# Two attentions with all products over 128 rows and contiguous operands, and rows of maxima turned on DVE

## The chip, the core and the metric

The kernel runs on one core of a Trainium2 chip. The core has a matrix engine (TensorE; PE in the profile, PEld for its weight loads), a vector engine (DVE), a scalar engine (ACT), a third elementwise engine (POOL) and SP, which only issues DMAs here. Each works through its own instructions in order and waits for the others by semaphores. A matmul multiplies a stationary operand (its weights, loaded by an instruction of its own) by a moving one and writes to a PSUM bank of 128 x 512 float32. The metric is the time of one execution in microseconds on the device; lower is better.

## What is computed

Two layers of an encoder over 512 tokens of width 1024, all in float32. Each layer runs two attentions beside a pooling branch, gates and merges the three, and ends with a gated MLP of width 2816. What matters here are the attentions:

```python
def block_attention(q, k, v):
    ...
    scale = dk ** -0.5
    ...
    def one_block(qi):
        sc = jnp.einsum('bqgrd,bkgd->bgrqk', qi, k, preferred_element_type=jnp.float32) * scale
        p = jax.nn.softmax(sc, axis=-1).astype(v.dtype)
        return jnp.einsum('bgrqk,bkgv->bqgrv', p, v)
...
    # MLA: 8 heads of 64 + 32 features, keys' 32 rotary features shared by the heads
    q = jnp.concatenate([q[..., :MLA_NOPE], apply_rope(q[..., MLA_NOPE:], cos, sin)], axis=-1)
    k = jnp.concatenate([k[..., :MLA_NOPE], apply_rope(k[..., MLA_NOPE:], cos, sin)], axis=-1)
    o = block_attention(q, k, v)
    # GQA: 8 heads of 64 features over 2 heads of keys and values
    q = apply_rope(rms_norm(q, qn_g), cos, sin)
    k = apply_rope(rms_norm(k, kn_g), cos, sin)
    o = block_attention(q, k, v)
```

GQA stands for the grouped-query attention and MLA for the latent one. So there are 16 heads a layer, each with a softmax over 512 keys for 512 queries.

## The kernel before, in words

**Precision.** TensorE works on a rounded form of float32 (the type fp32r). So an operand is split into a high part, written by ACT, and a low part, the difference, by DVE or POOL; a full product is the sum of three matmuls. Splitting the weights (`wh`, `wl` out of `raw`, 512 columns a piece) is most of POOL's work.

**Order.** The program writes the order of every engine's instructions out by hand. While it is built it keeps a clock (`Clock`) with a guessed cost for every instruction; `chain` puts the steps of a piece of work one behind the other in that clock, and `need` lets it run on until a result is ready. The clock decides nothing on the chip: it fixes which instruction stands before which on an engine, and in places which engine takes a piece (`pick`, `copy`). A changed cost of one step can so move other instructions too. Semaphores guard every true dependence.

**Stages.** In each layer the projections come first, then the GQA attention, then the MLA attention, then the output projection and the MLP. Products that don't depend on the attention (gates, branch projections, MLA's own q, k, v) are fed in between the attention's products as a filler, from a list in which each step of each head has its position (`PLAN`; four units are one head). `s_max` of a head stands up to about two units before its `probs`.

**A head.** Features lie over the rows (partitions), tokens over the 512 columns.

- `t_q`, `t_k` make the high and low parts of queries and keys. For GQA, `qa` holds the high part of a query head in its 64 rows and the low part in the other 64, `ka` the keys' high part twice, `kb` the keys' low part in rows 0 to 63 and ones in row 64, `qb` the queries' high part in rows 0 to 63. For MLA all are 96 rows high; `ka` has ones in row 96.
- `s_max` multiplies, for each of four blocks of 128 queries, the queries (as weights, every fourth column of `qa`) by all keys into the one bank `S`, and `red` on DVE takes the negative maximum over the keys into a column of `nm` (128 x 4). When the fourth is there, `row` moves the 512 numbers into one row of 512: row 64 of `qb` (GQA) or row 96 of `qa` (MLA), by a DMA issued from ACT's queue. The row of ones in the keys then subtracts the maximum inside the product of the scores.
- `probs`, for each of four blocks of 128 keys, makes the scores in a bank `ST` or `mi`: two matmuls for GQA (over 128 and 65 rows), three for MLA (96, 96 and 97 rows). Then come the exponential (ACT), the split into `ph` and `pl`, and a small rest (`vt`).
- `av_hi`, `av_lo`, `av_rest` multiply by the values into a bank `AV`; `o_out` normalizes.

**Turns.** MLA's queries and keys are made with tokens over the rows and must be turned. `block_turn` turns blocks of 32x32 on DVE (`turn_blocks`), writes them to DRAM (`put`) and reads them back in order (`get`: three DMAs of 64 KB for 96 features), both issued by SP. `mla_turn` does so for one head's queries (`tq`) or keys (`tk`); SP's queue carries the weights (`raw`) as well. The first turns of MLA are issued when the GQA attention has been written out.

**Buffers.** Most intermediate tiles are slots of 128 x 512 out of a ring of 47 (`slot`); small ones have buffers of their own (`small`).

Of the kernel before, what the change touches and what calls it, by code (L numbers as in the profile page):

```python
# [14 lines left out]
ALU = mybir.AluOpType  # L15
# [29 lines left out]
PLAN = {"gqa": (-4.2, -1.0, -0.2, 0.0, 0.65, 2.411, 4.57, 32.003),  # L45
        "mla": (-6.2, -2.9, -1.0, 0.1, 0.64, 1.678, 1.82, 35.5)}

D_ROW, D_OUT, D_IN, D_LAT = 3.4, 3.2, 4.0, 6.0
REST = 0.4
W_BIAS = 2.54  # L50
C_BIAS = 0.2
# [200 lines left out]


@with_exitstack
def trunk(ctx: ExitStack, tc: tile.TileContext, x, w, prm, gb, cst, out):
    nc = tc.nc
    ctx.enter_context(tc.manual_schedule())
    ck = Clock()
# [24 lines left out]
    def small(name, shape, dt=F32, bufs=2):  # L283
        uid[0] += 1
        t = sm.tile(shape, dt, tag=name, name=f"{name}_{uid[0]}", bufs=bufs)
        return t
# [22 lines left out]
    def f(ap):  # L309
        return ap.bitcast(F32)  # L310
# [226 lines left out]
    def layer(l, sq, xsrc):  # L537
# [12 lines left out]
        gcol = small("gcol", [P, 1], bufs=1)  # L550

        def tables():
            V.tensor_tensor(gcol[0:96], pr[0:96, PRM_MQ:PRM_MQ + 1], pr[0:96, PRM_MQ + 1:PRM_MQ + 2], ALU.mult)
            V.tensor_scalar(gcol[0:64], gcol[0:64], 96.0 ** -0.5, None, ALU.mult)
            V.tensor_scalar(gt[:, 0:128], gt[:, 0:128], 64.0 ** -0.5, None, ALU.mult)
            V.tensor_scalar(gt[:, 256:384], gt[:, 256:384], 96.0 ** -0.5, None, ALU.mult)
            for tb, o in zip(tabs, (0, 128)):
                for i, c0 in ((0, C_CG), (1, C_SG)):
                    G.tensor_tensor(
                        tb[:, 256 * i:256 * i + 256].rearrange("p (b f) -> p b f", b=4),  # L560
                        C[:, c0:c0 + 256].rearrange("p (b f) -> p b f", b=4),
                        bc(gt[:, None, o + 64 * i:o + 64 * i + 64], [P, 4, 64]), ALU.mult)
# [173 lines left out]
        def set_ones():  # L736
            for vh, _ in VG:
                V.memset(f(vh[:, :, 64:65]), 1.0)
            for _, kb in KAB:
                V.memset(f(kb[64:65, :T]), 1.0)  # L740

        at(14.0, set_ones)
# [190 lines left out]
        vm0 = small("vm0", [P, 4, 8])  # L933
        ss = small("ssm", [P, 2, 2, 4, 4])
        krr = small("krr", [P, 4, 32], bufs=1)
        kj_ = small("kj", [P, 4, 32], bufs=1)
        kss = small("kss", [P, 4], bufs=1)

        def rotary():
# [153 lines left out]

        turned = {}

        def block_turn(what, h, srcs, n):


            tr, to = slot("tr"), slot("tf")
            turned[what, h] = to  # L1100
            d = dp.tile([P, P * n], F32, tag=f"d{what}{l}{h}", name=f"d{what}{l}{h}")
            o = tr[:, :P * n].rearrange("p (j b t) -> p b j t", j=n, b=4)

            def turn_blocks():
                for b0, nb, src in srcs:
                    V.transpose(o[:, b0:b0 + nb], src.rearrange("p b (j f) -> p b j f", f=32))

            def put():
                SY.dma_start(d, tr[:, :P * n])
                ck.fin = ck.now + D_OUT  # L1110

            def get():
                for j in range(n):
                    SY.dma_start(to[32 * j:32 * j + 32, :T].rearrange("f (i c) -> f i c", i=4),
                                 d.rearrange("(i f) (j c) -> j f i c", i=4, j=n)[j])
                ck.fin = ck.now + D_IN
                done(what, l, h)

            return turn_blocks, put, get

        def mla_turn(what, h):
            m = (MQ if what == "tq" else MK)[h // 4]
            chain(([("mq" if what == "tq" else "mk", l, h // 4)], lambda: None),
                  *block_turn(what, h, [(0, 4, m[:, :, h % 4, :])], 3), after=0.0)


        def attention(kind, fill, okey, odst):
            gqa = kind == "gqa"
            hs, ot = {}, []
            kd = P if gqa else 96  # L1130

            def key(*k):
                return (kind, l) + k
# [1 line left out]
            def t_q(h):  # L1135
                if gqa:
                    return t_pair(h) if h % 2 == 0 else None
                s = hs.setdefault(h, {})
                need(("tq", l, h))
                qf = turned.pop(("tq", h))  # L1140
                qa, qb = s["qa"], s["qb"] = slot("qa", F32R), slot("qb", F32R)

                def lo():
                    G.tensor_tensor(qb[0:96, :T], qf[0:96, :T], f(qa[0:96, :T]), ALU.subtract)
                    done(*key("q", h))

                chain(lambda: A.activation(qf[0:96, :T], qf[0:96, :T], AF.Copy, scale=gcol[0:96]),
                      lambda: A.activation(qa[0:96, :T], qf[0:96, :T], AF.Copy), lo, after=0.0)

            def t_pair(h):  # L1150

                if h:
                    need(("tp", l, h))
                    tp = turned.pop(("tp", h))[:, :T]
                else:
                    tp = ps("mi")
                    for b in range(4):
                        need(("gqn", l, b))
                        turn(tp[:, b * P:b * P + P], gqo[b][:, :P])
                need(("kab", l))  # L1160
                steps = []
                for i in range(2):
                    s = hs[h + i] = {}
                    s["ka"], s["kb"] = KAB[h // 4]
                    qa, qb = s["qa"], s["qb"] = slot("qa", F32R), slot("qb", F32R)
                    own, other = slice(64 * i, 64 * i + 64), slice(64 - 64 * i, P - 64 * i)

                    def hi(qa=qa, own=own):
                        A.activation(qa[own, :T], tp[own], AF.Copy)

                    def lo(i=i, qa=qa, qb=qb, own=own, other=other):
                        (G if h else V).tensor_tensor(qa[other, :T], tp[own], f(qa[own, :T]), ALU.subtract)
                        if i == 1 and h == 0:
                            free("mi")
                        A.activation(qb[0:64, :T], qa[own, :T], AF.Copy)
                        done(*key("q", h + i))

                    steps.append((hi, lo))
                chain(steps[0][0], steps[1][0], steps[0][1], steps[1][1])
# [11 lines left out]
            def t_k(h):  # L1191
                if gqa:
                    return
                s = hs.setdefault(h, {})
                need(("tk", l, h))
                kf = turned.pop(("tk", h))
                ka, kb = s["ka"], s["kb"] = slot("kh", F32R), slot("kl", F32R)

                def hi():
                    G.memset(f(ka[96:97, :T]), 1.0)  # L1200
                    A.activation(ka[0:96, :T], kf[0:96, :T], AF.Copy)
                    done(*key("kh", h))

                def lo():
                    G.tensor_tensor(kb[0:96, :T], kf[0:96, :T], f(ka[0:96, :T]), ALU.subtract)
                    done(*key("kl", h))

                chain(hi, lo, after=0.0)

            def s_max(h, b):  # L1210
                s = hs[h]
                need(key("q", h))
                if not gqa:
                    need(key("kh", h))
                if b == 0:
                    s["nm"] = small("nm", [P, 4], F32R)
                sc = ps("S")
                mm(sc, s["qa"][0:kd, b:T:4], s["ka"][0:kd, :T], True, True)

                def red():  # L1220
                    V.tensor_reduce(s["nm"][:, b:b + 1], sc, AX.X, ALU.max, negate=True)
                    free("S")

                def row():
                    nc.scalar.dma_start(f((s["qb"][64:65] if gqa else s["qa"][96:97])[:, :T]), f(s["nm"]))
                    ck.fin = ck.now + D_ROW
                    done(*key("m", h))

                chain(red, *[row] * (b == 3))

            def probs(h, k):
                s = hs[h]
# [5 lines left out]
                kb_ = slice(k * P, k * P + P)  # L1238
                if gqa:
                    mm(sc, s["ka"][:, kb_], s["qa"][:, :T], True, False)  # L1240
                    mm(sc, s["kb"][0:65, kb_], s["qb"][0:65, :T], False, True)
                else:
                    mm(sc, s["kb"][0:96, kb_], s["qa"][0:96, :T], True, False)
                    mm(sc, s["ka"][0:96, kb_], s["qb"][0:96, :T], False, False)
                    mm(sc, s["ka"][0:97, kb_], s["qa"][0:97, :T], False, True)
                ph, pl = slot("ph", F32R), slot("pl", F32R)
                s["p", k] = (ph, pl)

# [477 lines left out]
```

## Time and profile before

| | |
|---|---|
| runs | 1580.4, 1580.51, 1582.9 us; median 1580.51 |
| the profiled execution | 1580.47 us, of it 1578.5 from the first to the last instruction (its span) |
| GQA attention, first and second layer | 106 to 238 us, 889 to 1021 us |
| MLA attention | 238 to 350 us, 1021 to 1132 us |
| DMA | 164.43 MB, 104 GB/s on the mean |

In the rows of the profile a group reads: line, engine, operation, written tile <- read tiles (for a matmul the moving operand, then the weights' tile), shapes, count | busy us in all, mean ns of one | idle us of the engine just before, and what ended it. The line is often that of a helper that records all operations of a kind. A matmul's duration counts its way through the array; the next one starts before it ends, so that 512-wide matmuls follow each other at some 0.23 us. A row of a timeline has the start and the length in us, then the instruction, and in brackets the idle time before it and what ended it. Stretches are listed as start and end, length, busy time (and number of instructions) of PE, PEld, DVE, ACT and POOL, granted clock, share of the DMA engines, GB/s.

### The profile page before, as it was taken

The numbers are of one execution on the slowest core, as the hardware profiler recorded it, in microseconds if no ns is written. First come the engines' busy times: TensorE is split into PE (matmuls) and PEld (weight loads), VectorE is DVE, ScalarE is ACT, GpSimd is POOL, SyncE is SP. The second block draws the span as 40 slices with busy tenths as digits, with TensorE's granted clock in tenths as the row PEclk, the third lists the DMA queues.
The fourth block names the chain that finished last, engine by engine and source line by source line (L and its number), as shares of the span: only waits on it lengthen the run. The fifth ranks groups of instructions, "written<-read, shape, count | busy, mean of one in ns | idle before, by whom it ended". The sixth has DMA issues, their size and how long they took to land.

```text
span 1578.5 us, 20363 instructions
## 1 busy us (share of the span) xinstructions
PE 1566.6 (99%) x7098; PEld 1310.3 (83%) x7098; DVE 952.9 (60%) x1360; ACT 787.4 (50%) x1426; POOL 1021.1 (65%) x890
## 2 busy tenths in 40 slices
PE   9999999999999999999999999999999999999999
PEld 8888888888888888888898888888888888888888
DVE  6877967866267776721047788678652777777000
ACT  6367866663444444432244677576534444444221
POOL 3864986854667667654577649868547766676542
PEclk9999999999999999999999999999999999999999
DMA  5432234314333233333334322343242223223331
GB/s 200 124 107 81 78 93 134 117 54 140 107 94 100 94 98 96 102 108 124 106 100 129 106 74 78 102 139 104 68 152 94 90 96 102 94 96 105 120 113 48
DMA packets 85927, 164.43 MB, mean 104 GB/s; under 512 B 25025, under 2 KB 47041, under 8 KB 85825
## 3 DMA queue, kind: packets, MB, share of 16 engines
q1 hardware_dynamic: 80928, 162.93, 33.3%
q8 instruction: 56, 0.92, 0.2%
q10 hardware_dynamic: 4896, 0.21, 0.2%
q14 instruction: 47, 0.38, 0.1%
HBM read 149.41 MB, written 13.63 MB: 103 GB/s over the span
## 4 chain that ended last, share of the span: by engine, by line
PE 87%; DVE 4%; POOL 2%; ACT 2%; issue 2%; DMA 2%; SPq 1%; POOLq 0%; ACTq 0%
PE ps_acc L367 39%; PE ps_AV L367 21%; PE ps_ST L367 21%; PE ps_S L367 3%; PE ps_mi L367 3%; DVE XM L223 1%; POOL wl L223 1%; DVE mgl L223 1%; ACT mgh L216 1%; POOL win L223 1%; SPq L713 1%; DVE gt L227 0%; DMA tf<-dtq 0%; ACT wh L216 0%; DMA tf<-dl 0%
## 5 line engine op out<-in xcount | busy, mean ns | idle before, releaser
L223 POOL TENSOR_TENSOR wl<-raw,wh 128x512 fp32r<-128x512 f32 (+2 forms) x503 | 674.2, 1352 | 413.3 <-ACT wh L216 374.4
L216 ACT ACTIVATE wh<-raw 128x512 fp32r<-128x512 f32 (+1 forms) x521 | 308.5, 607 | 124.8 <-PE ps_ST L367 42.0
L227 DVE SCALAR_TENSOR_TENSOR a<-u,prm,a 128x511 f32<-128x511 f32 x176 | 242.5, 1379 | 89.2 <-ACT a L216 84.3
L367 PE MATMUL ps_acc<-HH,wh 128*128 128x512 f32 x592 | 231.9, 392 | 0.5 <-DVE gt L223 0.5
L367 PE MATMUL ps_acc<-HH,wl 128*128 128x512 f32 x592 | 231.3, 391 | 0.0
L367 PE MATMUL ps_acc<-HL,wh 128*128 128x512 f32 x592 | 231.3, 391 | 0.0
L367 PEld LDWEIGHTS ps_acc<-HH,wl 128*128 128x128 f32 x592 | 111.3, 188 | 23.6
L367 PEld LDWEIGHTS ps_acc<-HH,wh 128*128 128x128 f32 x592 | 111.6, 188 | 23.0 <-issue 0.9
L367 PEld LDWEIGHTS ps_acc<-HL,wh 128*128 128x128 f32 x592 | 111.4, 188 | 22.9
L367 PE MATMUL ps_AV<-HH,wh 128*128 128x512 f32 x288 | 112.4, 390 | 0.0
L367 PE MATMUL ps_AV<-HH,wl 128*128 128x512 f32 x288 | 112.2, 390 | 0.0
L367 PE MATMUL ps_AV<-HL,wh 128*128 128x512 f32 x288 | 112.2, 390 | 0.0
L223 POOL TENSOR_TENSOR al<-a,ah 128x512 fp32r<-128x512 f32 x44 | 57.9, 1316 | 83.5 <-ACT ah L216 78.8
L231 DVE TENSOR_REDUCE nm<-ps_S 128x1 fp32r<-128x512 f32 x128 | 87.7, 685 | 37.5 <-PE ps_S L367 35.6
L367 PE MATMUL ps_ST<-HH,wh 128*128 128x512 f32 x240 | 93.7, 390 | 0.0
L367 PE MATMUL ps_ST<-HL,wh 128*128 128x512 f32 x240 | 93.5, 390 | 0.0
L367 PE MATMUL ps_ST<-HH,wl 128*128 128x512 f32 x240 | 93.5, 389 | 0.0
L216 ACT ACTIVATE ah<-a 128x512 fp32r<-128x512 f32 x44 | 27.8, 632 | 127.8 <-DVE a L223 127.8
L216 ACT ACTIVATE a<-u,prm 128x512 f32<-128x512 f32 x88 | 71.0, 809 | 27.0 <-DVE u L223 26.5
L216 ACT ACTIVATE a<-a 128x512 f32<-128x512 f32 x44 | 27.8, 632 | 106.2 <-DVE a L227 106.2
L216 ACT ACTIVATE HH<-XM,prm 128x512 fp32r<-128x512 f32 x32 | 23.1, 722 | 104.4 <-DVE XM L223 53.9
L216 ACT ACTIVATE ps_ST<-ps_ST 128x512 f32<-128x512 f32 x86 | 49.9, 581 | 39.8 <-PE ps_ST L367 38.0
(376 smaller groups left out, 3734.1 us busy)
## 6 DMA issues: line engine op xcount, KB each, us to landing
raw<-w SPq DMA_DIRECT2D x228, 512.0 KB, 3.5
raw<-w SPq DMA_DIRECT2D x13, 384.0 KB, 3.1
XM<-x SPq DMA_DIRECT2D x16, 256.0 KB, 4.2
dtq<-tr SPq DMA_DIRECT2D x16, 192.0 KB, 3.9
dtk<-tr SPq DMA_DIRECT2D x16, 192.0 KB, 4.0
tf<-dtq SPq DMA_DIRECT2D x48, 64.0 KB, 2.1
tf<-dtk SPq DMA_DIRECT2D x48, 64.0 KB, 2.4
raw<-w SPq DMA_DIRECT2D x6, 448.0 KB, 3.4
```

The costliest lines, as they stand in the source:

```text
L216: return self.eng.activation(out, in_, func, **k)
L223: return self.eng.tensor_tensor(out, *a)
L227: return self.eng.scalar_tensor_tensor(out, *a)
L231: return self.eng.tensor_reduce(out, in_, *a, **k)
L367: PE.matmul(o, lhsT=lhsT, rhs=rhs, start=start, stop=stop)
L713: SY.dma_start(to[32 * c:32 * c + 32, :T].rearrange("f (g t) -> f g t", t=32), src[4 * j + c])
```

## The change

- Contiguous weights: block b of `s_max` takes the 128 neighbouring columns b*128 to b*128+127 of `qa` in place of every fourth one.
- Full rows: every product of the attentions runs over 128 rows. The rows that had not been there are filled: for MLA the turns read 32 more rows from a new input `pad` (zeros for queries; a row of ones and 31 of zeros for keys) by one more DMA each, and all passes over 96 rows become passes over 128, where `gcol`, the scale per row, is first set to 1; the memset of the row of ones in `ka` goes. For GQA, rows 64 to 127 of `kb` are zeroed once a layer ahead of the ones, and rows 64 to 127 of `qb` by a memset on POOL for each head.
- Row of maxima: `lie` turns `nm`, each number repeated 32 times, in blocks of 32x32 on DVE into `nmt` (128 x 128), so that every group of 32 rows holds 128 of the maxima on each row; then `row` copies the four groups to 32 rows of `qb` or `qa`, two on ACT and two on DVE. The DMA is gone; all 32 rows hold the maxima, and only one of them meets a key row that isn't zero.
- `kj`, a small tile, becomes a slot; the clock's constant for the DMA goes.

```diff
-D_ROW, D_OUT, D_IN, D_LAT = 3.4, 3.2, 4.0, 6.0
+D_OUT, D_IN, D_LAT = 3.2, 4.0, 6.0
...
+            V.memset(gcol, 1.0)
...
+                V.memset(f(kb[64:P, :T]), 0.0)
                 V.memset(f(kb[64:65, :T]), 1.0)
...
-        kj_ = small("kj", [P, 4, 32], bufs=1)
+        kj_ = slot("kj2")[:, :P].rearrange("p (b f) -> p b f", b=4)
...
-        def block_turn(what, h, srcs, n):
+        def block_turn(what, h, srcs, n, rest=None):
...
+                if rest is not None:
+                    SY.dma_start(to[32 * n:P, :T], rest)
                 ck.fin = ck.now + D_IN
...
-            m = (MQ if what == "tq" else MK)[h // 4]
+            m, rest = (MQ[h // 4], pad[0]) if what == "tq" else (MK[h // 4], pad[1])
...
-                    G.tensor_tensor(qb[0:96, :T], qf[0:96, :T], f(qa[0:96, :T]), ALU.subtract)
+                    G.tensor_tensor(qb[:, :T], qf[:, :T], f(qa[:, :T]), ALU.subtract)
...
-                chain(lambda: A.activation(qf[0:96, :T], qf[0:96, :T], AF.Copy, scale=gcol[0:96]),
-                      lambda: A.activation(qa[0:96, :T], qf[0:96, :T], AF.Copy), lo, after=0.0)
+                chain(lambda: A.activation(qf[:, :T], qf[:, :T], AF.Copy, scale=gcol),
+                      lambda: A.activation(qa[:, :T], qf[:, :T], AF.Copy), lo, after=0.0)
...
+                    G.memset(f(qb[64:P, :T]), 0.0)
...
-                    G.memset(f(ka[96:97, :T]), 1.0)
-                    A.activation(ka[0:96, :T], kf[0:96, :T], AF.Copy)
+                    A.activation(ka[:, :T], kf[:, :T], AF.Copy)
...
-                    G.tensor_tensor(kb[0:96, :T], kf[0:96, :T], f(ka[0:96, :T]), ALU.subtract)
+                    G.tensor_tensor(kb[:, :T], kf[:, :T], f(ka[:, :T]), ALU.subtract)
...
-                    s["nm"] = small("nm", [P, 4], F32R)
+                    s["nm"] = small("nm", [P, 4])
                 sc = ps("S")
-                mm(sc, s["qa"][0:kd, b:T:4], s["ka"][0:kd, :T], True, True)
+                mm(sc, s["qa"][:, b * P:b * P + P], s["ka"][:, :T], True, True)
...
+                nmt = small("nmt", [P, P], bufs=1) if b == 3 else None
+
+                def lie():
+                    V.transpose(nmt.rearrange("p (b t) -> p b t", t=32), bc(s["nm"].unsqueeze(2), [P, 4, 32]))
+
                 def row():
-                    nc.scalar.dma_start(f((s["qb"][64:65] if gqa else s["qa"][96:97])[:, :T]), f(s["nm"]))
-                    ck.fin = ck.now + D_ROW
+
+                    o = (s["qb"][64:96] if gqa else s["qa"][96:P])[:, :T].rearrange("p (b g t) -> p b g t", b=4, t=32)
+                    for g in range(4):
+                        n = nmt[32 * g:32 * g + 32].rearrange("p (b t) -> p b t", t=32)
+                        if g < 2:
+                            A.activation(o[:, :, g], n, AF.Copy)
+                        else:
+                            V.tensor_tensor(o[:, :, g], n, n, ALU.max)
                     done(*key("m", h))
 
-                chain(red, *[row] * (b == 3))
+                chain(red, *[lie, row] * (b == 3))
...
-                    mm(sc, s["kb"][0:65, kb_], s["qb"][0:65, :T], False, True)
+                    mm(sc, s["kb"][:, kb_], s["qb"][:, :T], False, True)
                 else:
-                    mm(sc, s["kb"][0:96, kb_], s["qa"][0:96, :T], True, False)
-                    mm(sc, s["ka"][0:96, kb_], s["qb"][0:96, :T], False, False)
-                    mm(sc, s["ka"][0:97, kb_], s["qa"][0:97, :T], False, True)
+                    mm(sc, s["kb"][:, kb_], s["qa"][:, :T], True, False)
+                    mm(sc, s["ka"][:, kb_], s["qb"][:, :T], False, False)
+                    mm(sc, s["ka"][:, kb_], s["qa"][:, :T], False, True)
...
+        "pad": np.stack([np.zeros((32, T), np.float32), np.eye(32, 1, dtype=np.float32) * np.ones(T, np.float32)]),
```

More of the change, by code (lines that the diff above doesn't have):

```diff
@@ L254, in trunk @@
 @with_exitstack
-def trunk(ctx: ExitStack, tc: tile.TileContext, x, w, prm, gb, cst, out):
+def trunk(ctx: ExitStack, tc: tile.TileContext, x, w, prm, gb, cst, pad, out):
     nc = tc.nc
@@ L1121, in mla_turn @@
         def mla_turn(what, h):
-            m = (MQ if what == "tq" else MK)[h // 4]
+            m, rest = (MQ[h // 4], pad[0]) if what == "tq" else (MK[h // 4], pad[1])
             chain(([("mq" if what == "tq" else "mk", l, h // 4)], lambda: None),
-                  *block_turn(what, h, [(0, 4, m[:, :, h % 4, :])], 3), after=0.0)
+                  *block_turn(what, h, [(0, 4, m[:, :, h % 4, :])], 3, rest), after=0.0)
         def attention(kind, fill, okey, odst):
@@ L1129, in attention @@
             hs, ot = {}, []
-            kd = P if gqa else 96
             def key(*k):
```

## The prediction

> **What bounds the kernel now.** I read the cores view first, then the page's engine totals, then the busy times stretch by stretch. MLA and GQA stand for the latent and the grouped-query attention.
>
> ```profile
> core 0: 1578.5 us, clock 0.999
> PE 1566.6 (99%) x7098; PEld 1310.3 (83%) x7098; DVE 952.9 (60%) x1360; ACT 787.4 (50%) x1426; POOL 1021.1 (65%) x890
> 0.00:106.00 106.00, 101.68 (x497) 87.82 (x498) 83.82 (x153) 55.98 (x120) 67.70 (x64) 0.98 0.49 145
> 106.00:238.00 132.00, 131.73 (x599) 110.86 (x597) 100.82 (x177) 94.26 (x178) 92.95 (x113) 1.00 0.29 88
> 238.00:350.00 112.00, 110.63 (x478) 90.83 (x478) 85.46 (x144) 75.14 (x137) 78.57 (x74) 1.00 0.35 103
> ```
>
> The columns after each stretch's length are PE, weight loads, DVE, ACT and POOL. The clock is full, so nothing is to be had there. TensorE is the bound: 131.73 of the 132 us of the first layer's GQA stretch, 110.63 of 112 in MLA. There a matmul that takes TensorE a few ns longer lengthens the kernel by those ns, while work of the others lies beside it as long as it is not late. DVE is nearest to late: 85.46 of 112 us leave it 26.5 us, 3.3 per head.
>
> Next I looked at what single products and single weight loads take, shape by shape.
>
> ```profile
> L367 PE MATMUL ps_acc<-HH,wl 128*128 128x512 f32 x592 | 231.3, 391 | 0.0
> L367 PE MATMUL ps_S<-ka,qa 128*128 128x512 f32 x64 | 26.3, 412 | 0.0
> L367 PE MATMUL ps_S<-kh,qa 96*128 96x512 f32 x64 | 25.7, 401 | 0.4 <-DVE nm L231 0.4
> L367 PE MATMUL ps_AV<-ph,vm 128*128 128x512 f32 x64 | 25.6, 400 | 0.2 <-DVE ph L239 0.2
> L367 PE MATMUL ps_ST<-qb,kb 65*128 65x512 f32 x44 | 17.5, 397 | 0.0
> L367 PE MATMUL ps_ST<-qa,ka 128*128 128x512 f32 x44 | 17.2, 392 | 0.0
> L367 PE MATMUL ps_ST<-qa,kh 97*128 97x512 f32 x42 | 16.7, 398 | 0.0
> L367 PE MATMUL ps_ST<-qb,kh 96*128 96x512 f32 x42 | 16.7, 398 | 0.0
> L367 PE MATMUL ps_ST<-qa,kl 96*128 96x512 f32 x42 | 16.7, 396 | 0.0
> ...
> L367 PEld LDWEIGHTS ps_S<-ka,qa 128*128 128x128 f32 x64 | 19.8, 310 | 2.6
> L367 PEld LDWEIGHTS ps_S<-kh,qa 96*128 96x128 f32 x64 | 19.8, 310 | 3.5 <-DVE nm L231 0.8
> L367 PEld LDWEIGHTS ps_ST<-qa,ka 128*128 128x128 f32 x44 | 8.5, 192 | 1.2
> L367 PEld LDWEIGHTS ps_ST<-qb,kh 96*128 96x128 f32 x42 | 8.0, 190 | 1.8
> ...
> 159.80 0.29 PE L367 MATMUL ps_acc<-wh,ctl 128*128 128x256 f32 x1
> 159.92 0.50 PE L367 MATMUL ps_S<-ka,qa 128*128 128x512 f32 x1
> 160.26 0.39 PE L367 MATMUL ps_AV<-ph,vg 128*128 128x512 f32 x1
> ```
>
> The loads of the maxima's products (ps_S) take 310 ns, all others some 190, with 96 rows or 128: the odd thing about them is that they read every fourth column of qa. Part of that shows in the products: 412 and 401 ns against 392 of the full, contiguous product of the same operands (ps_ST<-qa,ka). It shows most behind a short matmul, which cannot cover a long load: the one at 159.92 holds the next back until 160.26, 0.34 us, where whole 512-wide products follow each other after 0.23. The products over 65, 96 and 97 rows take 396 to 398, 4 to 6 more than that full one.
>
> **The change part by part.** *Contiguous queries in the maxima* (128 products): 64 x (412 - 392) + 64 x (401 - 392) ns = 1.9 us less. *Full rows in the scores*: four kinds of 64 products each (those that go to ps_mi make up the 64): 64 x (5 + 4 + 6 + 6) ns = 1.3 us less. Together -3.2 us, all on the path. Bounds: against the 391 of the long stream, rounded to 390, it would be 64 x (22 + 11 + 7 + 6 + 8 + 8) = 4.0 us; and if the surplus is what any product of the attentions pays, for which the 400 of ps_AV<-ph,vm speaks, only 64 x (12 + 1) = 0.8 remains. I take the middle, since its 392 is the same operands in the same stage.
>
> The Trainium skill speaks against the second term: "TensorE: Matmul & The Clock Gate", section "LDWEIGHTS (loading the stationary operand)", has the load depend on the columns and not on the rows, and its closing table has a 32-row matmul take the time of a 128-row one; by it the padding is worth 0, not 1.3 us. For loads the trace agrees (190 with 96 rows, 192 with 128); for products it shows those 4 to 6 ns.
>
> *Row of maxima.* Gone are a DMA of 4-byte pieces per head, its issue on ACT's queue and its landing:
>
> ```profile
> L1225 ACTq DMA_DIRECT2D qa<-nm x16: 476/477/477, 246.3 to 1115.5; - x16
> qa<-nm ACTq DMA_DIRECT2D x16, 2.0 KB, 1.9
> L247 DVE STREAM_TRANSPOSE tr<-gqr 128x128 f32<-128x128 f32 x24 | 5.3, 274 | 0.0
> L223 DVE TENSOR_TENSOR vm<-ps_acc,vm 128x4 f32<-128x4 f32 x16 | 1.8, 152 | 0.0
> L227 DVE SCALAR_TENSOR_TENSOR vg<-ps_acc,rt,vg 128x126 fp32r<-128x126 f32 x4 | 1.4, 346 | 0.0
> L216 ACT ACTIVATE oinv<-oinv 32x16 f32<-32x16 f32 x32 | 6.8, 214 | 0.5
> L216 ACT ACTIVATE gkn<-ps_acc,rt 128x128 f32<-128x128 f32 x4 | 1.5, 368 | 2.6 <-PE ps_acc L367 2.6
> L251 POOL MEMSET kh<- 1x512 f32 x16 | 8.3, 521 | 0.9
> L251 DVE MEMSET kb<- x4: 485/485/485, 67.8 to 850.8; 1x512 f32 x4
> ```
>
> In its place DVE gets a 128x128 turn (0.274) and two copies of 32x128, between 152 and 346 ns each, nearer to the latter's 126 columns: some 0.3. That is 0.87 us per head, 28 us over 32 heads. ACT gets two copies between 214 and 368 ns, again some 0.3 each, for the 0.477 that the issue took: +0.1 per head. All three copies' engines are in order, so a late turn holds up the exponentials queued behind ACT's copies; the same queue waited for the same last maximum before, at its DMA issue. The shorter way (about 0.9 us instead of 1.9 to landing) frees nothing at once: PE hardly idles in these stretches, and a head's first scores are planned two quarter-heads behind its last maximum, 7 us at MLA's 112 / 8 = 14 us a head. Beside PE, 0.87 fits in DVE's 3.3 idle us per head, so I cost it at 0; without that cover it is the slow rival below. POOL: one memset of 64x512 more per GQA head (0.52 like the one-row memset, at most a full pass of 1.4), one fewer per MLA head; hidden in 39 idle us of the GQA stretch. DVE's memsets of kb grow from one row to 64 besides (four more, 1.9 us in all) in a stretch where it idles 22 of 106 us; uncovered, 1.9. The 96-row passes on ACT and POOL keep their 512 columns, so their time. The memset of gcol, the pad input and the square moved to a slot cost nothing I can see.
>
> *The pad rows of the MLA turns.* SP issues one more DMA (64 KB, 32 rows of 2 KB) after the three of every turn, 32 in all.
>
> ```profile
> 238.28 1.32 SPq L1114 DMA_DIRECT2D tf<-dtq  x3
> 239.71 1.31 SPq L1114 DMA_DIRECT2D tf<-dtk  x3
> 1022.62 1.27 SPq L1114 DMA_DIRECT2D tf<-dtq  x3
> 1024.00 1.31 SPq L1114 DMA_DIRECT2D tf<-dtk  x3
> 242.58 0.72 ACT L216 ACTIVATE tf<-tf,gcol 96x512 f32<-96x512 f32 x1 [3.70 <-DMA tf<-dtq]
> 1025.57 0.72 ACT L216 ACTIVATE tf<-tf,gcol 96x512 f32<-96x512 f32 x1 [3.53 <-DMA tf<-dtq]
> PE ps_acc L367 <- DVE vm L223: 1.5, 2, 0.8
> ```
>
> An issue takes 1.31 / 3 = 0.44 us. At each MLA start ACT stands 3.5 to 3.7 us for the first query turn; behind it wait the copies of the value products, whose DVE halves then hold PE (1.5 us in two waits, the last row). A fourth DMA lands there 0.44 later than the third, unless that one is slow: in the first layer the third was issued until 239.60 and landed only at 242.58, so a fourth, issued until 240.04, is hidden if it lands as fast as the second layer's third did, 1.7 us after its issue; in that second layer (1023.89 to 1025.57) it is late by its issue. I take 0.15 + 0.45 = +0.6 us. Bounds: 0, and 3 x 0.44 = 1.3 when the key turn, now two issues later, holds something too. Weight loads behind these issues on SP go out up to 0.9 later; there are three of them ahead.
>
> Sum: -3.2 + 0.6 = -2.6 on the profiled execution's 1580.47 (span 1578.5), so 1577.9; the median of the runs, 1580.51, is the same within 0.04.
>
> **The rivals.** *Rows are free:* only the stride pays, -1.9 + 0.6 = -1.3, 1579.2. For it: the 400 of ps_AV<-ph,vm, a product over full rows; against it, that qa,ka takes 392 with full rows among the very same neighbours. (The rule of the skill's page named above would give this time.)
>
> *The stride is not the cause of the 310:* then the change does not do what it says, and -1.3 + 0.6 gives 1579.8. Against it: both attentions have 310, with different rows.
>
> *DVE becomes late (slower).* ps_S is a single bank, so a late maximum holds the next product:
>
> ```profile
> 314.49 0.39 PE L367 MATMUL ps_acc<-HH,wl 128*128 128x512 f32 x1
> 315.27 0.62 PE L367 MATMUL ps_S<-kh,qa 96*128 96x512 f32 x1 [0.39 <-DVE nm L231]
> 315.73 0.39 PE L367 MATMUL ps_AV<-pl,vm 128*128 128x512 f32 x1
> ```
>
> Between 314.49 and 315.73 two products took 1.24 us, 0.78 over 2 x 0.23. That happens in one MLA head today. The turn and copies take a quarter of DVE's idle time, and the order of all instructions, written by the program's own clock, is made anew around them, as is the ring of slots. Four such waits more eat the gain; eight, in half of the 16 MLA heads, make 8 x 0.78 - 2.6 = +3.6: 1584.1. Against it: 3.3 idle us per head.
>
> *The new order loses a wait:* that one 0.78 and half of the 1.5 at the MLA starts go: -2.6 - 1.5 = -4.1, 1576.4. For it: ACT no longer holds 32 issues; against it: nothing aims at these waits.
>
> **How the numbers follow.** 0.2% is 3.2 us, about what a measurement of this kernel tells from no change. Forecast 0.40, of which 0.18 beyond -3.2 and 0.22 within; rows free 0.08; stride not the cause 0.03 (both within); DVE late 0.27, of which 0.24 beyond +3.2; a wait lost 0.22 (faster). Faster 0.40, same 0.36, slower 0.24. The forecast's own range is 0.8 to 4.0 less and 0 to 1.3 more: 1576.5 to 1581.0. The stated range, 1575.3 to 1584.5, holds the other cases too.
>
> **What would show it.** Loads of ps_S near 190; their products and the scores near 392; no issue by ACT; DVE near 92 us in the MLA stretch. Wrong on rows: scores still 396 to 398. Wrong on DVE: waits of ps_S for nm in several heads. Wrong on the turns: PE's waits for vm unlike 1.5 + 0.6.

## The result, and the profile after

The changed kernel takes 1601.43 us (median of four runs, 1600.93 to 1605.03) against 1580.95 of the kernel before beside it: a ratio of 1.0134, 95% interval 1.0119 to 1.0148. It is 20.5 us slower; the prediction said 2.6 us faster and had its slow end at 1584.5. The profiled execution took 1600.93 us.

The first fence has the changed kernel's cores view, its engine totals, and its busy times by stretch (after start, end and length: PE, weight loads, DVE, ACT, POOL, each with its number of instructions, then granted clock, DMA share, GB/s); the second has the same stretches of the kernel before.

```profile
core 0: 1599.1 us, clock 0.998
PE 1567.8 (98%) x7098; PEld 1300.8 (81%) x7098; DVE 998.6 (62%) x1455; ACT 811.4 (51%) x1497; POOL 1021.9 (64%) x890
106.00:242.00 136.00, 131.33 (x593) 107.47 (x593) 108.73 (x199) 100.32 (x195) 95.41 (x119) 1.00 0.29 86
242.00:365.00 123.00, 114.48 (x490) 91.79 (x489) 100.47 (x169) 80.39 (x154) 76.00 (x68) 0.97 0.35 103
365.00:850.00 485.00, 484.70 (x2162) 403.60 (x2161) 241.07 (x274) 194.13 (x339) 304.84 (x229) 1.00 0.34 105
1026.00:1150.00 124.00, 117.25 (x514) 94.76 (x513) 101.92 (x173) 85.95 (x164) 78.05 (x71) 1.00 0.39 115
```

```profile
106.00:242.00 136.00, 135.73 (x619) 114.34 (x618) 104.15 (x186) 95.14 (x179) 96.95 (x118) 1.00 0.30 91
242.00:365.00 123.00, 121.63 (x526) 99.77 (x525) 87.75 (x144) 81.76 (x149) 82.58 (x77) 1.00 0.34 100
1026.00:1150.00 124.00, 123.36 (x537) 101.97 (x536) 87.92 (x144) 81.67 (x150) 83.14 (x77) 1.00 0.34 106
```

TensorE, which had no time to spare, now stands idle: 4.67 us instead of 0.27 in the stretch from 106, 8.52 instead of 1.37 from 242, 6.75 instead of 0.64 from 1026. DVE's busy time in an MLA stretch goes up by 13 to 14 us. In the long stretch between the layers' attentions nothing changed.

What the change did to the products themselves is seen in the groups by shape (mean ns of one behind the busy time):

```profile
L367 PE MATMUL ps_S<-ka,qa 128*128 128x512 f32 x64 | 25.4, 398 | 2.1 <-DVE nm L231 1.7 <-POOL qa L223 0.3
L367 PE MATMUL ps_S<-kh,qa 128*128 128x512 f32 x64 | 25.4, 397 | 0.0
L367 PE MATMUL ps_AV<-ph,vm 128*128 128x512 f32 x64 | 24.9, 389 | 0.0
...
L367 PE MATMUL ps_ST<-qa,kl 128*128 128x512 f32 x42 | 16.8, 401 | 4.5 <-DVE qa L223 4.5
L367 PE MATMUL ps_ST<-qa,kh 128*128 128x512 f32 x42 | 16.4, 390 | 0.0
L367 PE MATMUL ps_ST<-qb,kh 128*128 128x512 f32 x42 | 16.4, 390 | 0.0
...
L367 PEld LDWEIGHTS ps_S<-kh,qa 128*128 128x128 f32 x64 | 12.1, 190 | 3.7 <-DVE nm L231 0.8
L367 PEld LDWEIGHTS ps_S<-ka,qa 128*128 128x128 f32 x64 | 12.0, 187 | 6.6 <-DVE nm L231 3.2 <-POOL qa L223 0.9
```

The loads of the maxima's products fell from 310 to 187 and 190 ns, the scores that don't wait from 398 to 390. So TensorE got what it was to get. The loss stands in the idle time behind the bars: `ps_ST<-qa,kl`, the first score product of an MLA head, waits 4.5 us for DVE's `qa`. Who writes that `qa` is the row of maxima; its instructions in the changed kernel (durations ns min/median/max, first and last start):

```profile
L247 DVE STREAM_TRANSPOSE nmt<-nm x32: 289/302/315, 113.5 to 1135.3; 128x128 f32<-128x128 f32 x32
L223 DVE TENSOR_TENSOR qb<-nmt x32: 282/286/1355, 113.9 to 1003.9; 32x128 fp32r<-32x128 f32 x32
L216 ACT ACTIVATE qb<-nmt x32: 307/308/312, 114.3 to 1003.6; 32x128 fp32r<-32x128 f32 x32
L223 DVE TENSOR_TENSOR qa<-nmt x32: 284/1152/1350, 253.7 to 1137.2; 32x128 fp32r<-32x128 f32 x32
```

The turn (302 ns, priced at 274) and ACT's copies (308) are nearly as priced. DVE's copies are of two kinds: some 285 ns, or up to 1355. One pair in time, first DVE, then POOL, then PE of the changed kernel:

```profile
278.12 0.30 DVE L247 STREAM_TRANSPOSE nmt<-nm 128x128 f32<-128x128 f32 x1
...
279.24 0.74 DVE L227 SCALAR_TENSOR_TENSOR vt<-ps_ST,vm,vt 128x512 fp32r<-128x512 f32 x1
280.02 1.93 DVE L223 TENSOR_TENSOR qa<-nmt 32x128 fp32r<-32x128 f32 x2
281.97 0.75 DVE L227 SCALAR_TENSOR_TENSOR vt<-ps_mi,vm,vt 128x512 fp32r<-128x512 f32 x1
```

```profile
279.20 1.30 POOL L223 TENSOR_TENSOR wl<-raw,wh 128x512 fp32r<-128x512 f32 x1 [0.39 <-ACT wh L216]
280.45 1.34 POOL L223 TENSOR_TENSOR XM<-XM,gt 128x512 f32<-128x512 f32 x1
```

```profile
280.89 0.40 PE L367 MATMUL ps_acc<-HH,wl 128*128 128x512 f32 x1
282.09 0.47 PE L367 MATMUL ps_ST<-qa,kl 128*128 128x512 f32 x1 [0.80 <-DVE qa L223]
```

The two copies end at 281.95, right after the second of POOL's instructions (280.45 + 1.34 = 281.79), and the product that reads their row starts 0.14 us later; TensorE has lost 0.97 us (1.20 from start to start less the usual 0.23). Of all 64 DVE copies, 18 have no POOL instruction beside them and take 282 to 289 ns. Of the 46 that have one, 25 are long (632 to 1355 ns), and every one of the 25 ends 143 to 153 ns after a POOL instruction has ended. The only short ones wholly inside a POOL instruction are four beside a memset. A copy that is already running when POOL's subtraction starts is not held either: the six of that kind take 284 to 289 ns.

That gives the waits of the changed kernel (us in all, times, longest):

```profile
ACT tf L216 <- DMA tf<-pad: 12.1, 4, 6.1
...
PE ps_ST L367 <- DVE qa L223: 4.5, 4, 1.4
PEld ps_AV L367 <- DVE pl L223: 4.2, 3, 2.0
PE ps_acc L367 <- DVE vm L223: 4.0, 2, 2.9
...
PE ps_mi L367 <- DVE qa L223: 3.5, 3, 1.7
```

The first and the fourth row lie at the MLA starts and are taken up below.

### The profile page after: what moved, and what is told of

Read it like the earlier page. It is cut to its first block, busy times and chain, and to the rows that moved or that the text cites. A ratio compares the mean times of both kernels' runs of the same rounds, so it can differ in the third digit from the quotient of the medians.

```text
span 1599.1 us, 20576 instructions
## 1 busy us (share of the span) xinstructions
PE 1567.8 (98%) x7098; PEld 1300.8 (81%) x7098; DVE 998.6 (62%) x1455; ACT 811.4 (51%) x1497; POOL 1021.9 (64%) x890
## 4 chain that ended last, share of the span: by engine, by line
PE 80%; DVE 10%; ACT 4%; DMA 2%; issue 2%; POOL 1%; SPq 1%; POOLq 0%; ACTq 0%; DVEq 0%
PE ps_acc L367 33%; PE ps_AV L367 21%; PE ps_ST L367 20%; PE ps_mi L367 3%; PE ps_S L367 3%; DVE XM L223 1%; DMA raw<-w 1%; DVE qa L223 1%; DVE pl L223 1%; DVE nm L231 1%; DVE mgl L223 1%; POOL wl L223 1%; DVE vt L227 1%; DVE gt L227 1%; ACT mgh L216 1%
## 5 line engine op out<-in xcount | busy, mean ns | idle before, releaser
L231 DVE TENSOR_REDUCE nm<-ps_S 128x1 f32<-128x512 f32 x128 | 87.0, 680 | 31.6 <-PE ps_S L367 31.1
```

Of the source, the lines that this page charges most:

```text
L231: return self.eng.tensor_reduce(out, in_, *a, **k)
```

## The experiments

Three theories, of which more than one can hold. *A, the copies:* DVE's copies, which name `nmt` twice as an input, are held up by POOL, and scores and later work wait. *B, the pads:* the fourth DMA of every MLA turn makes the start of MLA late. *C, the order:* the program's clock, with new guesses, writes another order, and that order is worse by itself. Ratios are to the kernel before, timed beside it (medians 1581.09, 1580.47 and 1579.74 us in the three groups of runs).

**e1_reduce_copies.** One word of the changed kernel is another; every engine's order stays the same.

```diff
-                            V.tensor_tensor(o[:, :, g], n, n, ALU.max)
+                            V.tensor_reduce(o[:, :, g], n.unsqueeze(3), AX.X, ALU.max)
```

> The changed kernel with its two DVE copies of the row made by a one-source TENSOR_REDUCE over a last dimension of 1 in place of TENSOR_TENSOR max(n, n); the clock's costs and so the order of all instructions stay as they are. Theory A (the two-source copies are held up by POOL, 0.28 us when free, 1.15 to 1.35 when POOL is at work; 40.6 us over 64 copies where 18 would do, and PE waits behind them): the copies take 0.25 to 0.3 us each and some 10 to 15 us of the 20 come back, 1586 to 1591. Theory B (the pad DMAs at the turns): no more than 4 us back, 1597 or above. Theory C (the order the clock writes when it thinks the row comes 2.4 us sooner): no more than 5 us back, 1596 or above.

Measured: 1587.53 us, ratio 1.0045 (1.0028 to 1.0061), 14 us less than the changed kernel. The copies, beside the same POOL:

```profile
L231 DVE TENSOR_REDUCE qb<-nmt x32: 277/280/281, 113.3 to 996.1; 32x128 fp32r<-32x128 f32 x32
...
L231 DVE TENSOR_REDUCE qa<-nmt x32: 278/280/283, 252.6 to 1123.4; 32x128 fp32r<-32x128 f32 x32
```

With one input instead of two, all 64 take 277 to 283 ns, 47 of them with a POOL instruction beside them, and TensorE has no wait for a copy on DVE any more. Theory A is shown, and some 6.5 us of the loss are not its. The edit changes the instruction as well as the number of its inputs. The changed kernel's own trace parts the two: its `pl<-ps_ST,ph`, a TENSOR_TENSOR with one input in PSUM, starts 62 times inside a POOL TENSOR_TENSOR and takes 629 to 692 ns there, 652 to 693 without. So it is not the instruction as such that is held.

**e2_pads_dma_row.** Full rows and pads as in the changed kernel; the row of maxima by the old DMA, and so the strided weights.

```diff
-                mm(sc, s["qa"][:, b * P:b * P + P], s["ka"][:, :T], True, True)
+                mm(sc, s["qa"][:, b:T:4], s["ka"][:, :T], True, True)
...
+                    nc.scalar.dma_start(f((s["qb"][64:65] if gqa else s["qa"][96:97])[:, :T]), f(s["nm"]))
+                    ck.fin = ck.now + D_ROW
```

> Full rows and pad DMAs as in the changed kernel, but the row of maxima by DMA and every fourth column as weights, as before (the clock's 3.4 us with it). Theory A: 1578 to 1583, loads of ps_S at 310 ns, score products at 390 to 392. Theory B: most of the loss stays, 1592 or above. Theory C: 1578 to 1583 too.

Measured: 1582.75, ratio 1.0011 (1.0002 to 1.0021). So neither full rows nor pads make the 20 us. But the pads are not free: in e2 the first query turn at the MLA start of layer 1 is asked for at the same time as before (238.13, before 238.28) and lands 1.4 us later:

```profile
239.50 0.43 SPq L1119 DMA_DIRECT2D tf<-pad  x1
...
243.97 0.72 ACT L216 ACTIVATE tf<-tf,gcol 128x512 f32<-128x512 f32 x1 [5.42 <-DMA tf<-pad]
```

In before that instruction of ACT started at 242.58. TensorE's idle time there grows from 0.99 to 2.40 us, and in layer 2 from 0.80 to 0.48 + 1.05.

**e5_turn_no_pads** and **e6_turn_reduce_no_pads.** The kernel before with contiguous weights and the new row of maxima, but the old 96, 65 and 97 rows and no pads (the square stays in its slot); e5 copies with two inputs, e6 with one.

```diff
-                mm(sc, s["qa"][0:kd, b:T:4], s["ka"][0:kd, :T], True, True)
+                mm(sc, s["qa"][0:kd, b * P:b * P + P], s["ka"][0:kd, :T], True, True)
...
-                chain(red, *[row] * (b == 3))
+                chain(red, *[lie, row] * (b == 3))
```

> The kernel before with contiguous weights and the row by the DVE turn and the four copies (two-source on DVE), without full rows and without pad DMAs. Theory A: most of the loss, 1592 to 1600, DVE copies at 0.8 to 1.2 us on the mean in MLA. Theory B: near 1580. Theory C: as A.

> As the run without full rows and pads, but with the one-source copies on DVE; same order. Theory A: 1578 to 1585, since neither held-up copies nor pad DMAs are left. Theory B: near 1580 as well. Theory C: 1592 or above, since the order stays.

Measured: e5 1589.28, ratio 1.0055 (1.004 to 1.007); e6 1586.44, ratio 1.0034 (1.002 to 1.0047). Both miss what A had forecast (1592 to 1600 and 1578 to 1585). Without full rows the second input costs 2.8 us, with them 14. Two differences may account for that, and no run parts them: with full rows the first of an MLA head's three score products already reads the row, here only the third; and here fewer copies are long (19 instead of 25; median of `qa` 289 ns, up to 1864). Neither padded nor unpadded does the kernel come back to 1581, so something that both share costs some 5 us. It lies in the first layer's GQA, which in these four kernels that have the turn takes 3.5 to 4.8 us longer than before (table below for two of them). There SP's queue differs. First the kernel before, then e1 (`x4` puts a run of like issues into one row):

```profile
120.89 16.04 SPq L321 DMA_DIRECT2D raw<-w  x3
138.09 0.33 SPq L1109 DMA_DIRECT2D dtp<-tr  x1
143.49 0.33 SPq L321 DMA_DIRECT2D raw<-w  x1
```

```profile
120.85 23.50 SPq L321 DMA_DIRECT2D raw<-w  x4
144.44 0.38 SPq L1111 DMA_DIRECT2D dtp<-tr  x1
...
148.45 0.69 DVE L223 TENSOR_TENSOR pl<-ps_ST,ph 128x512 fp32r<-128x512 f32 x1 [2.91 <-DMA dtp<-tr]
```

In e1 the put of a turned block (`dtp<-tr`) stands behind a fourth load of weights, which cannot go until POOL has freed its buffer. The put goes out 6.35 us later, its source keeps its slot of the ring as long, and DVE's next `pl`, which is given that slot, waits 2.91 us for it. The program's clock, with other instructions on DVE and ACT to account for, had written the two past each other. Right behind that `pl` TensorE stands still for 1.2 us; four more waits of TensorE in that stage of e1, 3.6 us together, are not traced to the put.

**f1, f3, f4: that order undone.** In e1, e6 and the changed kernel the GQA's first planned turn is due a little earlier; in the chip's trace of f1 the put is back ahead of the fourth load, at 138.72. On SP only this put and one later load of weights change places, but the clock also moves some 80 of TensorE's 7098 products and as many of DVE's instructions, so it is one order against another and not the put alone.

```diff
-PLAN = {"gqa": (-4.2, -1.0, -0.2, 0.0, 0.65, 2.411, 4.57, 32.003),
+PLAN = {"gqa": (-4.5, -1.0, -0.2, 0.0, 0.65, 2.411, 4.57, 32.003),
```

> The changed kernel with the two DVE copies of the row of maxima as reductions of one operand (as in the first of these runs, 1587.5 us), and the due time of the window attention's first row set from -4.2 to -4.5 us, so that SP's order has the turned probabilities' transfer ahead of the fourth weight load again, as the kernel before had it. Theory C (the order of SP's queue costs the layer-1 window attention some 5 us): about 1582, between 1580 and 1584, and DVE's wait of 2.9 us for the turned row in that attention is gone. Rival (the rest of the loss sits in the pads and in the copies that remain): 1586 or more, whatever the order.

> The kernel before with contiguous weights and the DVE turn with one-operand copies, without full rows and pads (1586.4 us in the run before), with the due time -4.5. Theory C: 1580 to 1582, about the kernel before, as the contiguous weights' gain is paid for by the copies' wait ahead of the third product. Rival (order no cause): 1586 again.

> The changed kernel itself, two-operand copies kept, with the due time -4.5 alone. If the copies (theory A) and the order (theory C) add up: 1601.4 less some 5, 1595 to 1597. If the order's loss is a consequence of the late copies: 1600 or more.

Measured: f1 1583.8, ratio 1.0019 (1.0009 to 1.0028); f3 1581.89, 1.0008 (0.9998 to 1.0017); f4 1596.48, 1.0101 (1.0086 to 1.0116). The changed kernel, e1 and e6 give back 5.0, 3.7 and 4.5 us. Theory C is shown for the order as a whole: e1's idle time of TensorE in the first layer's GQA falls from 6.2 to 1.3 us in f1. How much of it was the put alone is not shown. The price of C adds to that of A: f4 to f1, the copies alone in the mended order, is 12.7 us.

**f2_pads_behind_put.** f1 with the pad rows' DMA issued right behind the put, ahead of its landing; the other engines' order is that of f1.

```diff
                 SY.dma_start(d, tr[:, :P * n])
+                if rest is not None:
+                    SY.dma_start(to[32 * n:P, :T], rest)
...
-                if rest is not None:
-                    SY.dma_start(to[32 * n:P, :T], rest)
                 ck.fin = ck.now + D_IN
```

> The run before this one (reductions of one operand, due time -4.5), with the transfer of the pad rows issued right behind the put of the turned row instead of behind the gets that follow its landing; every computing engine keeps its order. Theory B (the pad's late landing delays the first attention product of each MLA layer, 2 to 3 us in a layer): 1577 to 1579, and TensorE's idle time ahead of the first MLA product falls from 3 us to about 1. Rival (the pads' landing hides behind the gets of the keys): within 1 us of the run before it.

Measured: 1582.98, ratio 1.001 (0.9997 to 1.0024): 0.8 us under f1, which the intervals don't tell apart. Theory B's 1577 to 1579 did not come. The idle time at the first MLA start stayed: 2.77 us from start to start at 243.0, against 0.99 at 244.6 in the kernel before. Both come out of it at about the same time, 243.0 + 0.23 + 2.77 = 246.00 here and 244.6 + 0.23 + 0.99 = 245.82 there. f2's TensorE comes 1.6 us sooner and waits 1.8 longer. SP and ACT of f2:

```profile
236.94 0.33 SPq L321 DMA_DIRECT2D raw<-w  x1
237.36 1.33 SPq L1118 DMA_DIRECT2D tf<-dtq  x3
...
242.77 0.72 ACT L216 ACTIVATE tf<-tf,gcol 128x512 f32<-128x512 f32 x1 [5.73 <-DMA tf<-dtq]
```

The gets of the second head's query go out behind a load of weights that POOL lets go only at 236.9, and land at 242.8, 5.4 us after the first of them was issued. ACT waits 5.73 us for them, and behind it in its queue stand the copies of the value products that TensorE needs. So there is a theory D: this landing sets the start of MLA, and whatever TensorE gains ahead of it is given back there.

**i1, i2, i4, i5: the gets ahead of that load.** The clock is told that the second head's put lands sooner (after 2.0 us in f2, the kernel before and f3; 1.4 us in f2 for i5). SP then has the gets of the query before that load of weights; in i5's first layer those of the key too.

```diff
-                ck.fin = ck.now + D_OUT
+                ck.fin = ck.now + (2.0 if h == 1 else D_OUT)
```

> The run with one-operand reductions, due time -4.5 and pads behind the puts (f2: 1582.98 us), in which the planner is told that the put of the second head's turned rows lands after 2.0 instead of 3.2 us; SP's order then has that head's three gets of the query ahead of the weight load that waits for POOL to free its buffer. In f2 the MLA's first products resume at 245.8 us, in before at 245.6: whatever TensorE gains up to there is given back to a landing that starts only when that weight load is let go. Theory D (that landing swallows the gain at both MLA starts): the idle time there falls from 2.8 and 1.5 us to 1 or less and the time to 1579 to 1580.5, level with or below the kernel before. Rival (the idle time is that of the PSUM bank or of ACT's own work): within 1 us of 1583.

> The kernel before with the same 2.0 us for the second head's put and nothing else, as the control for the run ahead of it. Theory D: before's own idle time at the MLA starts (0.99 and 0.80 us) goes, 1579 to 1580.5. Rival: no change, 1580.5, or slower where the moved weight load is missed.

> The run without full rows and pads with due time -4.5 (f3: 1581.89 us), with the second head's put at 2.0 us. Theory D: the idle time of 1.9 us at the first MLA start goes, 1580 to 1581. Rival: 1582 as before.

> As the first of these runs with 1.4 us in place of 2.0, which in layer 1 puts the gets of the key ahead of that weight load too. Theory D: 1578.5 to 1580, as the key's landing no longer waits for the weight load either. Rival (the moved weight load is then itself late): 1582 or more.

Measured: i1 1577.83, ratio 0.9987 (0.9979 to 0.9996); i2 1579.07, 0.9994 (0.9986 to 1.0003); i4 1578.01, 0.9992 (0.9983 to 1.0001); i5 1579.2, 1.0004 (0.9995 to 1.0013). SP and ACT of i1:

```profile
234.04 1.28 SPq L1118 DMA_DIRECT2D tf<-dtq  x3
237.15 0.35 SPq L321 DMA_DIRECT2D raw<-w  x1
...
237.12 0.72 ACT L216 ACTIVATE tf<-tf,gcol 128x512 f32<-128x512 f32 x1
```

The gets go out 3.3 us sooner, ACT has no wait left in front of `tf`, and TensorE's idle time there falls from 2.77 us, and 0.87 more ahead of the next score product, to 0.32 ahead of the latter. i1 beats both kernels: its median is 23.6 us below the changed one's (of another group of runs), and its ratio to the one before is 0.13% under 1 (0.04 to 0.21%). Theory D is shown for the first layer; in the second the gets are moved elsewhere and the idle time at the MLA start only goes from 1.45 and 0.87 us to 1.11 and 0.86. The clock moves other instructions here too (some 90 products on TensorE), so the 3.3 us at the MLA start are the part that is seen to be the landing's. The kernel before, which stood there for 0.99 us only, gains nothing that can be told (i2). i5's median lies where D had it, but 1.4 us above i1's; its profiled execution, one of its slower ones, has 0.55 us of idle time at 241.4 and 0.94 at 253.2 that i1 has not.

Two of these runs say what the change itself is worth, and the comparison with the kernel before alone hides it. i2 is the kernel before with the same early gets: i1 is 1.2 us below it (1576.39 to 1578.96 us in its eleven runs against 1577.87 to 1583.19). And i4, which has the contiguous weights and the turn with one-input copies but neither full rows nor pads, comes out at 1578.01, not to be told from i1's 1577.83 (both lower than D had them). So no gain of the full rows can be told in the whole time.

The stages of the profiled executions (us, each from the first maxima's product of GQA, of MLA, or the first product with the merged gate, to the next of these):

| | before | changed | e1 | f4 | f1 | f2 | i1 |
|---|---|---|---|---|---|---|---|
| GQA, layer 1 | 129.76 | 133.88 | 133.21 | 128.75 | 128.18 | 128.04 | 128.08 |
| MLA, layer 1 | 152.88 | 162.61 | 156.95 | 161.86 | 157.32 | 155.02 | 150.57 |
| merge and MLP, to layer 2's GQA | 500.44 | 500.06 | 499.85 | 500.13 | 503.49 | 500.84 | 499.75 |
| GQA, layer 2 | 129.83 | 130.21 | 129.67 | 130.36 | 129.73 | 129.71 | 129.65 |
| MLA, layer 2 | 151.34 | 158.09 | 151.72 | 158.36 | 153.35 | 151.80 | 153.56 |

Row by row: copies with two inputs cost 5.7 us in layer 1's MLA and 6.4 in layer 2's (changed less e1); the order 5.1 in layer 1's GQA (changed less f4); the early gets bring 4.4 in layer 1's MLA (f2 less i1). GQA of layer 1 with all mended is 1.7 us below before, but 0.7 of that is only moved: with full rows the order has 582 products between the two marks, before 585, and three more in MLA. The remaining 1.0 is gain of the products; in layer 2's GQA other waits eat it (idle time of TensorE 2.7 us in i1, 0.9 before). f1's 503.49 is of an execution that was the slowest of its ten; its median is 3.9 us under it.

## Why the prediction was wrong, point by point

*TensorE's gain: right, and undersized.* Predicted -3.2 us. I summed, over all neighbouring matmuls, the time from start to start above the usual one of their width, as far as it is under 60 ns: 9.55 us before, 4.25 in the changed kernel, so -5.3, a third more than the 4.0 I had for the upper end (with the usual time taken a little otherwise it is -4.9 to -5.4). e2, full rows alone, has 7.55; e6, contiguous weights alone, 7.80. The two together bring more than their sum (3.75), and the 400 of `ps_AV<-ph,vm`, which had spoken for "the surplus is what any product of the attentions pays", fell to 389 although nothing of that product was changed. It fell to 393 with full rows alone (e2) and to 395 with contiguous weights alone (e6), so part of its surplus came with its neighbours. This gain is TensorE's own; of the whole time, i1 against i2 shows 1.2 us.

The closing table of the Trainium skill's "TensorE: Matmul & The Clock Gate", section "Why this matters for your kernels", has a single product over 32 rows take the time of one over 128. For the products over 65, 96 and 97 rows here, 7.55 against 9.55 does not bear that out.

*DVE's copies: the step that failed.* I priced them "between 152 and 346 ns each, nearer to the latter's 126 columns: some 0.3". It was right for a copy that runs alone and up to 1 us too low for the others. The rows I took read PSUM. The copies read SBUF twice, and such rows stood in the profile of before, tiny shapes with huge times:

```profile
L223 DVE TENSOR_TENSOR pl<-ps_ST,ph 128x512 fp32r<-128x512 f32 x86 | 58.7, 683 | 12.8 <-ACT ph L216 11.8
...
L223 DVE TENSOR_TENSOR win<-win,C 128x8 f32<-128x8 f32 x16 | 8.3, 556 | 11.3 <-POOL win L223 11.3
...
L235 DVE TENSOR_SCALAR mx<-mx,ssc 128x256 f32<-128x256 f32 x8 | 6.9, 866 | 0.5 <-POOL ssc L223 0.5
...
L223 DVE TENSOR_TENSOR fac<-fac,C 128x16 f32<-128x16 f32 x4 | 5.0, 1253 | 12.1 <-POOL fac L223 12.1
```

Sixteen columns in 1253 ns, or eight in 556, are no price of columns, where `pl<-ps_ST,ph`, with one input in PSUM, takes 683 for 512. An upper bound of 1.25 per copy would have followed from them: 2 x 1.25 + 0.27 = 2.8 us a head against the 3.3 of idle DVE, which leaves next to no cover.

The Trainium skill names the part that the two share: "VectorE: DVE Perf Modes", section "Two Vector instructions with no wait between them", has an instruction with two SBUF inputs read one of them through an interface that it shares with GpSimd. The trace agrees, and adds the price: a held copy ends some 0.15 us after POOL's instruction.

*"Beside PE, 0.87 fits in DVE's 3.3 idle us per head, so I cost it at 0."* A mean over a head covers no work that has a due time. What the copies write is read by the next score product, and with full rows by the first of the three; e5 to e6 (2.8 us) against changed to e1 (14) fits that, though fewer copies are long in e5. That a head's maxima stand two quarter-heads ahead of its scores in the plan was not 7 us of slack on the chip: in the fences above the turn of `nm` ran at 278.12 and the scores were due at 281.12 (280.89 + 0.23), 3.0 us later.

*The rival "DVE becomes late" (0.27)* had the engine and the direction right, not why DVE would be late, and missed place and size. It put eight waits of 0.78 us on the bank `ps_S`. There the changed kernel has 1.7 us in two; most sit at `ps_ST` and `ps_mi` for `qa` (8.0 us in seven waits) and at `ps_AV` for `pl`.

*The pads: +0.6, bounds 0 to 1.3.* e2 shows +1.4 in layer 1, where I had 0.15, and +0.7 in layer 2, where I had 0.45: a fourth DMA in the row lands later than by the length of its issue. Taking it out of the row (f2) brought only 0.8 us, and what I had not seen at all is that the MLA start waits for a landing whose issue is held by the weight load ahead of it. Of TensorE's gain before that place, 1.6 us, nothing came out of it until i1 moved the issue. I had looked at the queue behind the gets ("Weight loads behind these issues"), not ahead of them.

*The order: priced at nothing.* I wrote that the order "is made anew around them, as is the ring of slots", and gave it no term. It cost 3.7 to 5.0 us in one stage. Two neighbours on SP's queue and a slot that stayed held are the part of it that the traces show; which other moved instructions had a share stays open.

So the 20.5 us are: 5.0 of order and 12.7 of copies (changed to f4 to f1, medians), and 2.8 in which the gain of 5.3 is outweighed by the MLA starts and smaller waits. With the three mended the change comes to 1577.83. That this is the time forecast for it as it stood is chance: the early gets were no part of the change, and the kernel before with them is at 1579.07, so beside it the mended change is worth some 1.2 us and not the 2.6 forecast.

## What to carry to other kernels

An instruction's price depends on where its inputs lie and what runs beside it: take it from rows with the same kinds of operands, and look for tiny shapes with large times. Give a change its control: i1 and i2 differ by the mended change, i1 and the kernel before by the early gets as well. Work put into another engine's idle time needs a due time, not a mean. In a kernel whose order is written by a planner, compare the queues after an edit, that of the DMA issuer first; and a gain of the bounding engine is only kept if the next landing that it waits for moves too.

## What the runs showed of the hardware

A DVE copy of 32x128 as TENSOR_REDUCE, with one SBUF input, takes 277 to 283 ns in all 64 cases of e1. As TENSOR_TENSOR with two SBUF inputs it takes some 285 ns, unless POOL is in the middle of a TENSOR_TENSOR when it starts; then it ends no sooner than some 145 ns after POOL's, and a copy of 632 ns or more ends 143 to 153 ns after. A single SBUF tensor as input is no escape by itself: `mx<-mx,ssc`, a TENSOR_SCALAR of 128x256 with one such tensor and one number per row (in the rows of DVE before, above), takes 340 to 343 ns alone and 1378 to 1405 beside POOL's subtractions, in the kernel before as in the changed one, and there too it ends some 150 ns after POOL's. Inputs from PSUM show no such hold (`pl<-ps_ST,ph`).

After the longer idle time at the first MLA start the granted clock fell. The changed kernel, and f2 whose TensorE was idle nearly as long:

```profile
250.00:254.00 4.00, 1.20 (x3) 0.83 (x3) 2.09 (x7) 2.51 (x6) 2.98 (x5) 0.82 0.85 229
254.00:258.00 4.00, 2.99 (x7) 2.12 (x7) 2.45 (x4) 2.47 (x6) 2.12 (x2) 0.50 0.43 83
```

```profile
242.00:246.00 4.00, 1.39 (x7) 0.84 (x6) 1.02 (x5) 2.66 (x5) 1.77 (x4) 1.00 0.57 213
246.00:250.00 4.00, 3.30 (x14) 2.45 (x15) 2.71 (x6) 2.97 (x6) 3.33 (x3) 1.00 0.33 101
```

At 0.50 the products follow each other at 0.43 us instead of 0.23. In f1 (0.50 from 246 to 250) that held for ten products and more, at least 10 x 0.2 = 2 us, most of the 2.3 that parts it from f2 in the table's MLA of layer 1. In that layer it happened in all four kernels that stood there 2.87 us or longer (changed, e1, f1, f4) and in none that stood 2.77 or less. But in i1's second layer it came (granted clock 0.60 from 1026 to 1030) after 1.11 and 0.86 us with a few products between, where f2's 1.45 and 0.87 did nothing, so the length of one gap does not decide it alone. Seven products at 0.43 us there are 1.4 of the 1.8 us by which i1's last MLA row is above f2's.

The Trainium skill's "TensorE: Matmul & The Clock Gate", section "What's actually happening", has the rate fall to half after an idle window of some 3.4 us whose phase is free-running. The half rate agrees with the 0.50, and the free phase would fit what i1 and f2 show; the idle times here are shorter than that window.
